# One encoder layer on one core: a fourth buffer for raw weights, two private buffer groups dissolved into general ones, and a new table of stage times

## The chip, the cores and the metric

The kernel runs on one core of a Trainium2 chip. Its time is the device time of one execution in microseconds, as the median of several runs. The kernel before took 1064.9, 1064.27 and 1064.7 us in three runs, so its median is 1064.7 us.

## The reference

One layer of a bidirectional encoder, on 512 positions of 1024 channels, all in float32. Two branches mix the tokens and a gated feed-forward part (FFN) follows:

```python
h = rmsnorm(x, mix_norm)
p = h @ w_in                                    # 1024 -> 9248 columns
rx, ry, qkv, z, ba, gates = split(p)
y_rnn = rglru_branch(rx, ry, ...) @ w_rnn_proj  # 12 blocks of 128 channels: convolution,
                                                # gates r and i by 128x128 weights, scans both ways
y_dn = deltanet_branch(qkv, z, ba, ...) @ w_dn_proj  # 8 heads, both directions, chunks with a
                                                # triangular solve and a carried state
g_rnn, g_dn = split(sigmoid(gates))
x = x + (g_rnn * y_rnn + g_dn * y_dn) @ w_out
h = rmsnorm(x, ffn_norm)
gt, up = split(h @ w_gate_up)                   # 2 x 2816 columns
x = x + (silu(gt) * up) @ w_down
return rmsnorm(x, final_norm)
```

## The kernel before

**Products.** TensorE (PE) does float32 products as products of two parts: every operand is split into a rounded part `hi` and a rest `lo`, and a tile of 128 output columns is the sum of hi·hi, lo·hi and hi·lo, three matmuls for each 128 input channels. For a weight tile this costs a transfer into a raw buffer (tag `wraw`, `NW` buffers of 4 KB per partition), a cast on ScalarE (ACT) to `hi`, and a subtraction on VectorE (DVE) for `lo` (`stage`, `weights`, `weights_k`). The tiles `whi` and `wlo` have two buffers each.

**Stages.** The program text runs through 229 stages: the norm and its transposes; tiles of `w_in`; the 12 RG-LRU blocks (`rg_front`, `rg_exp`, `rg_rest`, `rg_out`); four pairs of DeltaNet heads, each with `dn_front`, `dn_mats`, `dn_inverse`, `dn_state`, `dn_z` and `dn_out`; the two projections (`rnn_part`, `dn_part`); `w_out` (`out_mm`); the FFN in 22 pairs of tiles, of which the last 20 use a scheme with seven products of quarter size in place of eight; and the down projection.

`dn_inverse(g)` inverts small triangular blocks of pair `g`: a long chain of small DVE operations on a tile `X`, ended by a transpose into `tb[1]`, a subtraction from the identity, and a transpose into `tb[0]`. Small 32x32 matmuls on PE wait for that last transpose.

`down_sums(j)` serves the seven-product scheme of the down projection: for each of 11 `j` it loads two blocks of `w_down`, makes two sums on DVE and writes the result to DRAM (`sums`), from which it is read again much later. Its operands `r` and `b22` are tiles of tags `bg` and `bgb`, with two buffers each. In `rg_front` the weights of the RG-LRU gates come into `graw`, which has a single buffer.

**What sets the order.** Nothing is issued as the text runs. Every operation goes through a `Rec` object into a `Plan`, which is why nearly all rows of the profile carry line L379, the recorder's own. `Plan.order()` then deals the operations out to the five engines' queues by a simulated list schedule. An operation's priority is the time of its stage, `TIMES[s]` in tenths of a microsecond, plus its offset within the stage (loads of weights are put 40 or 20 us before their use, casts and subtractions `AHEAD` = 12 us). The operation of lowest priority whose inputs are ready, and for whose tiles the tag has a free buffer, is placed next. Stages past the end of the list `TIMES` follow the last entry at a spacing given by `spend`. So both the numbers of `TIMES` and the numbers of buffers (`N2` of 2 KB, tag `t2`; `N4` of 4 KB, tag `t4`; `NW`) decide the order on every engine, and the order is fixed when the program is built. On the chip each engine runs its list strictly in that order and waits where an input or a buffer isn't there.

Of the kernel before, what the change touches and what calls it, by code (L numbers as in the profile page):

```python
# [8 lines left out]
F32R = mybir.dt.float32r  # L9
# [5 lines left out]
P = 128  # L15
# [17 lines left out]
RELEASE = 200  # L33
LOOK = 40
TIMES = [
# [10 lines left out]
]  # L46
ENGINES = ("PE", "DVE", "ACT", "POOL", "SP")
N2, N4, NW = 14, 22, 3
AHEAD = 12.0
LASTK = 3  # L50
GATES = (0, 2, 4, 6, 16)
# [333 lines left out]
def trunk(ctx: ExitStack, tc: tile.TileContext, x, mix_norm, w_in, rg_conv_w, rg_conv_b, rg_wa, rg_ba, rg_wx, rg_bx,  # L385
# [9 lines left out]
    wp = ctx.enter_context(tc.tile_pool(name="wp", bufs=2))  # L395
# [10 lines left out]
    def nm(s):  # L406
        uid[0] += 1
        return f"{s}{uid[0]}"

    def new(pool, shape, tag, bufs, dt=F32):  # L410
        return plan.tile(pool, shape, dt, tag, bufs, nm(tag))
# [4 lines left out]
    def axb():  # L416
        return new(ps, (P, 512), "ax", 3)
# [4 lines left out]
    def two(dt=F32, shape=(P, 512)):  # L422
        return new(t2, shape, "t2", N2, dt)

    def four(dt=F32, shape=(P, 2, 512)):
        return new(t4, shape, "t4", N4, dt)
# [7 lines left out]
    def act(out_, in_, func, after=(), **kw):  # L434
        plan.extra = after
        A.activation(out_, in_, func, **kw)
        plan.extra = ()
# [6 lines left out]
    def f(ap):  # L444
        return ap.bitcast(F32)
# [112 lines left out]
    def pcol(i, j):  # L558
        return par[:, i, j:j + 1]
# [77 lines left out]
    def in_proj(col, po=None, admit=()):  # L637
        spend(5.2)
        hi, lo = (weights_k if len(first_tiles) < 3 else weights)(win[:, :, col:col + P], KD, P, admit)
        po = mmb() if po is None else po  # L640
        mm3(po, hi, lo, lambda k: hh[:, k, :], lambda k: hl[:, k, :], KD, 2 if len(first_tiles) < 3 else 1)
        first_tiles.append(col)
        return po

    def split(src, pair):
        A.copy(pair[:, 0, :], src)
        V.tensor_tensor(pair[:, 1, :], src, f(pair[:, 0, :]), ALU.subtract)

    def conv(po, w, bias, u):
        A.activation(u, po, AF.Identity, scale=w(2), bias=bias)  # L650
        V.scalar_tensor_tensor(u[:, 2:S], po[:, 0:S - 2], w(0), u[:, 2:S], ALU.mult, ALU.add)
        V.scalar_tensor_tensor(u[:, 1:S], po[:, 0:S - 1], w(1), u[:, 1:S], ALU.mult, ALU.add)
        V.scalar_tensor_tensor(u[:, 0:S - 1], po[:, 1:S], w(3), u[:, 0:S - 1], ALU.mult, ALU.add)
        return u
# [79 lines left out]
    def rg_front(b):  # L734
        u, us, r, i = two(), four(F32R), four(), four()
        po = in_proj(C_RX + b * P, admit=(u, us, r, i))
        graw, ghi, glo = new(wp, (P, 4, P), "graw", 1), two(F32R, (P, 4, P)), two(F32R, (P, 4, P))
        now = plan.t
        plan.t = now - (40 if b > 2 else 12)
        Q.dma_start(graw[:, 0:2, :], wa[:, b])  # L740
        Q.dma_start(graw[:, 2:4, :], wx[:, b])
        plan.t = now - AHEAD
        A.copy(ghi, graw)
        V.tensor_tensor(glo, graw, f(ghi), ALU.subtract)
        plan.t = now
        conv(po, lambda k: rg_w(k, b), rg_b(b), u)
        split(u, us)
        for q in range(4):
            d = q % 2
            pq = axb()  # L750
            T.matmul(pq, ghi[:, q, :], us[:, 0, :], start=True, stop=False)
            T.matmul(pq, ghi[:, q, :], us[:, 1, :], start=False, stop=False)
            T.matmul(pq, glo[:, q, :], us[:, 0, :], start=False, stop=True)
            act((r if q < 2 else i)[:, d, :], pq, AF.Sigmoid, bias=pcol(0, (O_BA if q < 2 else O_BX) + 12 * d + b))
        V.tensor_tensor(i, i, u.unsqueeze(1).to_broadcast([P, 2, S]), ALU.mult)
        return r, i
# [373 lines left out]
    def rg_group(bs):  # L1130
        nonlocal prev
        fr, m0 = marks(lambda: [rg_front(b) for b in bs])
        rg_flush()
        hs, m2 = rg_mid(bs, fr, m0)
        prev = (bs, hs, m2)
# [26 lines left out]
    def down_sums(j, after):  # L1162

        now = plan.t
        r, b22 = new(wp, (P, 2, 512), "bg", 2), new(wp, (P, 512), "bgb", 2)
        plan.extra = after
        Q.dma_start(r, wdn[:, j, 0, :].rearrange("p (h n) -> p h n", h=2))
        Q.dma_start(b22, wdn[:, j, 1, 512:D])
        plan.extra = ()
        V.tensor_tensor(r[:, 0, :], r[:, 0, :], r[:, 1, :], ALU.add)  # L1170
        V.tensor_tensor(r[:, 1, :], r[:, 1, :], b22, ALU.add)
        sums[j] = new(dr, (P, 2, 512), "sums", NF // 2)
        Q.dma_start(sums[j], r)
        plan.t = now
# [223 lines left out]
    for n in range(BRIDGE, NF):  # L1398
        if n - BRIDGE < NF // 2:
            down_sums(n - BRIDGE, last_split)  # L1400
        gate_up(n)
# [222 lines left out]
```

## Time and profile before

| what | value |
|---|---|
| runs | 1064.9, 1064.27, 1064.7 us, median 1064.7 us |
| span of the profiled execution (the only time the page gives for it) | 1066.3 us |
| TensorE busy | 1045.2 us, 98% of the span, 6731 matmuls |
| VectorE busy | 867.6 us, 81% |
| ScalarE busy | 675.7 us, 63% |
| GpSimd busy | 53.0 us, 5% |
| moved by DMA | 122.83 MB |

The profiled execution is 1.6 us (0.15%) longer than the median of the runs. Tile names in the profile come without their numbers, so `t` is any general tile (tags `t2` and `t4`), `mm`, `ax` and `st` are the three kinds of PSUM banks, and `hh`, `hl` the two parts of the normed input. A row of a timeline gives a start, the time taken by so many like instructions, and in brackets how long the engine had idled before them and for what. A row of the chain of waits is a piece of the chain that ended last. A row of a table of windows gives the length of a stretch and each engine's busy time in it.

### The profile page before, as it was taken

What the parts mean: (1) busy time and instruction counts of PE and PEld (TensorE: products, weight loads), DVE (VectorE), ACT (ScalarE), POOL (GpSimd) and SP (SyncE); (2) the same over time, 40 slices, a digit from 0 to 9 for tenths busy, and PEclk for the clock granted to TensorE, in tenths of its full rate; (3) what the DMA queues carried; (4) which work ended last, traced back from release to release, by engine and by line L of the source; (5) the groups of instructions that cost most, each with busy time, mean ns of one, the idle gap of its engine ahead of it and who ended that gap; (6) DMA issues with size and microseconds to landing.
All of it is one profiled execution on the core that took longest, in us unless ns stands there. A gap on an engine that the chain in (4) does not pass through costs nothing.

```text
span 1066.3 us, 17661 instructions
## 1 busy us (share of the span) xinstructions
PE 1045.2 (98%) x6731; PEld 908.7 (85%) x6731; DVE 867.6 (81%) x1606; ACT 675.7 (63%) x1244; POOL 53.0 (5%) x109
## 2 busy tenths in 40 slices
PE   8999999999999999999999999999999999999997
PEld 7888888887879887988788898889999999998876
DVE  7679899669966696599379567669989989889998
ACT  7997997878464856783874534447444544546664
POOL 2000000202000211110020000000000000000000
PEclk9999999999999999999999999999999999999999
DMA  8142333224331243223203222554577433325643
GB/s 254 45 119 79 102 85 91 68 86 124 104 109 33 83 125 91 58 73 99 71 15 96 79 103 80 183 168 149 178 229 246 129 102 104 113 93 197 193 137 113
DMA packets 174390, 122.83 MB, mean 115 GB/s; under 512 B 5953, under 2 KB 160721, under 8 KB 174305
## 3 DMA queue, kind: packets, MB, share of 16 engines
q1 hardware_dynamic: 172832, 118.41, 37.1%
q10 hardware_dynamic: 1184, 3.15, 0.8%
q8 instruction: 53, 0.87, 0.3%
q0 software_dynamic: 288, 0.13, 0.1%
q14 instruction: 33, 0.26, 0.1%
HBM read 113.78 MB, written 7.90 MB: 114 GB/s over the span
## 4 chain that ended last, share of the span: by engine, by line
PE 71%; DVE 14%; ACT 8%; issue 4%; DMA 3%; POOL 0%; SPq 0%; DVEq 0%; ACTq 0%; POOLq 0%
PE mm L379 43%; PE ax L379 18%; PE st L379 10%; DVE t L379 9%; ACT t L379 5%; DVE wlo L379 3%; ACT L379 1%; DVE na L379 1%; ACT whi L379 1%; ACT ax L379 1%; DMA wraw<-sums 1%; DMA wraw<-in_w_in_dram 1%; DMA wraw<-in_w_gate_up_dram 1%; DMA bg<-in_w_down_dram 1%; DVE hl L379 0%
## 5 line engine op out<-in xcount | busy, mean ns | idle before, releaser
L379 DVE TENSOR_TENSOR t<-t,t 128x512 fp32r<-128x512 f32 (+23 forms) x466 | 226.7, 501 | 14.8 <-ACT t L379 6.3
L379 PE MATMUL mm<-hh,whi 128*128 128x512 f32 (+2 forms) x648 | 229.4, 363 | 0.4 <-ACT hh L379 0.4
L379 PE MATMUL mm<-hl,whi 128*128 128x512 f32 (+2 forms) x648 | 228.9, 362 | 0.8 <-DVE hl L379 0.8
L379 ACT CAST whi<-wraw 128x1024 fp32r<-128x1024 f32 (+3 forms) x139 | 130.1, 937 | 155.2 <-PE mm L379 87.8
L379 DVE TENSOR_TENSOR wlo<-wraw,whi 128x1024 fp32r<-128x1024 f32 (+3 forms) x138 | 150.4, 1092 | 75.1 <-PE mm L379 27.4
L379 PE MATMUL mm<-hh,wlo 128*128 128x512 f32 (+1 forms) x632 | 146.8, 364 | 0.0
L379 PE MATMUL ax<-t,t 32*32 32x32 f32 (+3 forms) x1062 | 141.7, 288 | 2.9 <-issue 1.8
L379 PEld LDWEIGHTS mm<-hl,whi 128*128 128x128 f32 (+1 forms) x648 | 121.8, 188 | 18.5 <-DVE hl L379 1.2
L379 PEld LDWEIGHTS mm<-hh,whi 128*128 128x128 f32 (+1 forms) x648 | 121.7, 188 | 17.8 <-ACT hh L379 0.7
L379 PEld LDWEIGHTS ax<-t,t 128*128 128x128 f32 (+1 forms) x1062 | 109.5, 162 | 20.9 <-issue 4.6
L379 PEld LDWEIGHTS mm<-hh,wlo 128*128 128x128 f32 x632 | 109.1, 190 | 17.4
L379 ACT CAST t<-t 128x512 fp32r<-128x512 f32 (+2 forms) x128 | 80.9, 650 | 48.2 <-DVE t L379 42.9
L379 DVE SCALAR_TENSOR_TENSOR t<-mm,par,t 128x511 f32<-128x511 f32 (+1 forms) x108 | 80.3, 745 | 20.3 <-ACT t L379 19.0
L379 PE MATMUL mm<-t,t 128*128 128x256 f32 (+1 forms) x468 | 91.6, 337 | 0.8 <-DVE t L379 0.7
L379 ACT ACT_TABLE_LOAD x69 | 88.5, 1283 | 5.2 <-PEq L1610 1.7
L379 PE MATMUL mm<-t,whi 128*128 128x512 f32 x320 | 82.1, 395 | 0.5 <-ACT whi L379 0.5
L379 PEld LDWEIGHTS mm<-t,t 128*128 128x128 f32 x468 | 72.4, 190 | 11.1 <-DVE t L379 2.5
L379 PEld LDWEIGHTS mm<-t,whi 128*128 128x128 f32 x320 | 59.3, 188 | 12.7 <-ACT whi L379 0.7
L379 ACT CAST t<-wraw 128x1024 fp32r<-128x1024 f32 (+1 forms) x51 | 44.9, 881 | 29.0 <-DMA wraw<-in_w_gate_up_dram 11.2
L379 ACT ACTIVATE t<-t 128x128 f32<-128x128 f32 (+4 forms) x86 | 47.1, 559 | 24.9 <-DVE t L379 23.6
L379 DVE TENSOR_TENSOR t<-wraw,t 128x1024 fp32r<-128x1024 f32 (+1 forms) x51 | 51.7, 1016 | 6.1 <-ACT t L379 5.9
L379 PE MATMUL mm<-t,wlo 128*128 128x512 f32 x160 | 43.3, 394 | 0.0
(210 smaller groups left out, 1702.9 us busy)
## 6 DMA issues: line engine op xcount, KB each, us to landing
wraw<-in_w_in_dram SPq DMA_DIRECT2D x72, 512.0 KB, 3.8
wraw<-in_w_gate_up_dram SPq DMA_DIRECT2D x44, 512.0 KB, 4.2
wraw<-in_w_rnn_proj_dram SPq DMA_DIRECT2D x16, 384.0 KB, 3.6
bg<-in_w_down_dram SPq DMA_DIRECT2D x11, 512.0 KB, 4.1
sums<-bg SPq DMA_DIRECT2D x11, 512.0 KB, 4.7
wraw<-sums SPq DMA_DIRECT2D x11, 512.0 KB, 4.6
wraw<-in_w_down_dram SPq DMA_DIRECT2D x22, 256.0 KB, 3.0
wraw<-in_w_down_dram SPq DMA_DIRECT2D x11, 512.0 KB, 3.7
```

What stands on the lines that cost most here:

```text
L379: self.plan.add(e, lambda: real(*a, **kw), outs, ins, cost, tail, table)
```

## The change

Three numbers of buffers change and the table `TIMES` is replaced. The weights of the RG-LRU gates (`graw`) become general 2 KB tiles, and the operands of the weight sums (`bg`, `bgb`) general 4 KB and 2 KB tiles. In SBUF this frees 2 KB + 2 x 4 KB + 2 x 2 KB = 14 KB per partition, and one more `wraw` buffer (4 KB), two more `t4` (8 KB) and one more `t2` (2 KB) take up 14 KB. The table before has 159 entries for 229 stages; the new one has 229.

```diff
 TIMES = [
-    -153745, -118892, -151742, -141630, -118601, -110624, -115268, -33958, -18020, -66486, -73432, -37443, -49540,
...
+    -193727, -159384, -193730, -126073, -120235, -159028, -125968, -63810, -13198, -66391, -64154, -63637, -49334,
...
 ]
 ENGINES = ("PE", "DVE", "ACT", "POOL", "SP")
-N2, N4, NW = 14, 22, 3
+N2, N4, NW = 15, 24, 4
...
     def rg_front(b):
         u, us, r, i = two(), four(F32R), four(), four()
         po = in_proj(C_RX + b * P, admit=(u, us, r, i))
-        graw, ghi, glo = new(wp, (P, 4, P), "graw", 1), two(F32R, (P, 4, P)), two(F32R, (P, 4, P))
+        graw, ghi, glo = two(shape=(P, 4, P)), two(F32R, (P, 4, P)), two(F32R, (P, 4, P))
...
     def down_sums(j, after):
 
         now = plan.t
-        r, b22 = new(wp, (P, 2, 512), "bg", 2), new(wp, (P, 512), "bgb", 2)
+        r, b22 = four(), two()
```

No operation is added or dropped: PE has the same number of matmuls in its list before and after. What changes is the order on all engines. Three places follow; the names are tiles, with the number of the tile in the program text.

**VectorE at the end of the inverse of pair 1.** `t2611` is `X`, `t2612` the product `tmp`, `t2614` is `tb[1]` and `t2613` is `tb[0]`; `wlo` with another number belongs to the weights of some product. Before:

```order
L379 TENSOR_TENSOR t2611_691<-t2611_691,t2612_692 128x15
L379 STREAM_TRANSPOSE t2614_694<-t2611_691 128x32x16
L379 TENSOR_TENSOR t2614_694<-id3256_136,t2614_694 128x512
L379 TENSOR_TENSOR wlo805_885<-wraw803_883,whi804_884 128x1024
L379 STREAM_TRANSPOSE t2613_693<-t2614_694 128x512
```

Now:

```order
L384 TENSOR_TENSOR wlo801_881<-wraw799_879,whi800_880 128x1024
L384 TENSOR_TENSOR t2611_691<-t2611_691,t2612_692 128x15
L384 STREAM_TRANSPOSE t2614_694<-t2611_691 128x32x16
L384 TENSOR_TENSOR t2614_694<-id3256_136,t2614_694 128x512
L384 TENSOR_SCALAR n2705_785<-dssq699_779 128x8
L384 STREAM_TRANSPOSE t2613_693<-t2614_694 128x512
```

The subtraction for a weight tile of 128x1024 that stood between the subtraction from the identity and the last transpose is gone from there; a scalar operation on 128x8 stands there now, and a subtraction for another weight tile stands a little ahead.

**VectorE in the last part of the DeltaNet projection, ahead of `w_out`.** `t490` to `t493` hold the merged branches, `wlo1065` and `wlo1068` are the low parts of the first tiles of `w_out`, `t41086` and `t41089` those of its second half. Before, the stretch reads

```order
L379 TENSOR_TENSOR t491_171<-t491_171,t21018_1098 128x512
L379 TENSOR_TENSOR t41089_1169<-wraw1087_1167,t41088_1168 128x1024
L379 TENSOR_TENSOR t41019_1099<-t491_171,t41019_1099 128x512
L379 TENSOR_TENSOR wlo1065_1145<-wraw1063_1143,whi1064_1144 128x1024
L379 TENSOR_TENSOR t41092_1172<-wraw1090_1170,t41091_1171 128x1024
```

and the first of the 22 additions of the weight sums (`bg1163_1243<-bg1163_1243`) comes 26 rows further on, among the last rows of `w_out`. Now (`t41163`, `t41188` and `t41212` are the `r` of three sums):

```order
L384 TENSOR_TENSOR t491_171<-t491_171,t21018_1098 128x512
L384 TENSOR_TENSOR t41163_1243<-t41163_1243 128x512
L384 TENSOR_TENSOR t41163_1243<-t41163_1243,t21164_1244 128x512
L384 TENSOR_TENSOR t41019_1099<-t491_171,t41019_1099 128x512
L384 TENSOR_TENSOR t492_172<-t492_172,t2844_924 128x512
L384 TENSOR_TENSOR wlo1065_1145<-wraw1063_1143,whi1064_1144 128x1024
L384 TENSOR_TENSOR t492_172<-t492_172,t2989_1069 128x512
L384 TENSOR_TENSOR t41188_1268<-t41188_1268 128x512
L384 TENSOR_TENSOR t492_172<-t492_172,t21036_1116 128x512
L384 TENSOR_TENSOR t41188_1268<-t41188_1268,t21189_1269 128x512
```

The additions of the first sums have moved from the end of `w_out` and the FFN to between the splits of the merged branches; a third pair (`t41212`) follows two rows after these, ahead of `wlo1068`.

**PE at its first products.** `mm62` is the small tile of 32 columns of `w_in` (both parts, 64 columns), `mm105` and `mm120` are full tiles of 128 columns, and `ax33` to `ax36` take transposes of the input. Before:

```order
L379 MATMUL ax35_115<-ident1_81,t428_108 128x128
L379 MATMUL mm62_142<-hh19_99,whi61_141 64x256
L379 MATMUL mm105_185<-hh19_99,t4103_183 128x256
L379 MATMUL mm62_142<-hl20_100,whi61_141 64x256
L379 MATMUL mm62_142<-hh19_99,whi61_141 64x256
L379 MATMUL mm62_142<-hl20_100,whi61_141 64x256
L379 MATMUL ax36_116<-ident1_81,t421_101 128x128
```

Now:

```order
L384 MATMUL ax35_115<-ident1_81,t428_108 128x128
L384 MATMUL mm120_200<-hh19_99,t4118_198 128x256
L384 MATMUL mm120_200<-hl20_100,t4118_198 128x256
L384 MATMUL mm120_200<-hh19_99,t4118_198 128x256
L384 MATMUL mm120_200<-hl20_100,t4118_198 128x256
L384 MATMUL ax36_116<-ident1_81,t421_101 128x128
```

The first products come from one full tile alone, where before a small tile and a full one took turns.

23 rows, old and new, of the table TIMES are left out of this document.

## The prediction, made before the changed kernel ran

> **What bounds the kernel now.** I read the page first for the busy shares, then the table of windows by 100 us for where TensorE (PE) is not busy, then PE's timeline and the chain of waits at those places, and VectorE's (DVE's) timeline where the wait is on DVE.
>
> The page's head and the windows (length; then busy time of PE, its weight loads, DVE, ACT, POOL; clock; DMA share; GB/s):
>
> ```profile
> span 1066.3 us, 17661 instructions
> PE 1045.2 (98%) x6731; PEld 908.7 (85%) x6731; DVE 867.6 (81%) x1606; ACT 675.7 (63%) x1244; POOL 53.0 (5%) x109
> ...
> 0.00:100.00 100.00, 94.22 (x520) 80.92 (x521) 78.45 (x131) 83.18 (x129) 7.39 (x21) 1.00 0.45 128
> ...
> 400.00:500.00 100.00, 97.91 (x714) 82.82 (x713) 76.49 (x201) 64.63 (x149) 11.12 (x24) 0.98 0.29 80
> 500.00:600.00 100.00, 97.98 (x869) 82.21 (x868) 72.15 (x181) 66.10 (x151) 5.42 (x14) 1.00 0.24 65
> 600.00:700.00 100.00, 100.00 (x563) 83.92 (x563) 60.27 (x114) 40.84 (x79) 0.00 (x0) 1.00 0.36 112
> 700.00:800.00 100.00, 98.10 (x732) 93.44 (x730) 92.58 (x160) 55.79 (x102) 0.00 (x0) 1.00 0.59 189
> ...
> 1000.00:1066.00 66.00, 58.55 (x263) 47.39 (x261) 60.12 (x98) 40.35 (x66) 0.00 (x0) 0.96 0.41 136
> ```
>
> PE is the bound: it is busy for 1045.2 of 1066.3 us, and the change removes none of its matmuls. Only the other 21.1 us can be won. Of these 5.8 lie in the first 100 us and 7.45 in the last 66 (the tail behind the last matmuls); 2.1, 2.0 and 1.9 lie in the windows from 400, 500 and 700. A new order cannot make PE's own work shorter, so I look only at these waits, and at what may make new ones.
>
> The largest wait is at the end of the inverse of DeltaNet pair 1. PE's rows there, the wait in brackets (378.26 is the last product of `dn_mats`, on which the inverse starts), then DVE's at the same place, then windows across it:
>
> ```profile
> 378.26 1.02 PE L379 MATMUL ax<-t 128*128 128x256 f32 x4
> ...
> 415.67 0.39 PE L379 MATMUL mm<-hl,whi 128*128 128x512 f32 x1
> 418.15 0.75 PE L379 MATMUL ax<-t,na 32*32 32x32 f32 x64 [2.09 <-DVE t L379]
> ```
>
> ```profile
> 415.64 0.69 DVE L379 TENSOR_TENSOR t<-id,t 128x512 f32<-128x512 f32 x1
> 416.25 1.22 DVE L379 TENSOR_TENSOR wlo<-wraw,whi 128x1024 fp32r<-128x1024 f32 x1
> 417.39 0.70 DVE L379 STREAM_TRANSPOSE t<-t 128x512 f32<-128x512 f32 x1
> ```
>
> ```profile
> 415.60:418.10 2.50, 0.45 (x3) 0.03 (x1) 2.46 (x4) 0.80 (x2) 0.00 (x0) 1.00 0.00 0
> ...
> 419.20:420.90 1.70, 1.70 (x6) 1.16 (x4) 0.00 (x0) 1.68 (x6) 0.00 (x0) 0.54 0.94 280
> 420.90:422.60 1.70, 1.70 (x67) 1.24 (x66) 0.00 (x0) 0.32 (x2) 0.00 (x0) 0.50 0.00 0
> ```
>
> PE stood 2.09 us for the last transpose, and DVE put a weight subtraction of 1.22 us ahead of that transpose. Afterwards the granted clock is 0.54 and 0.50 for 3.4 us.
>
> **The change part by part.** The unit of PE's work, from the chain (a run of 24 matmuls of 512 columns, and one of 12 with 256), and of DVE's additions of 512 elements:
>
> ```profile
> 52.35 5.44 PE st L379 x24
> ...
> 790.01 1.44 PE mm L379 x12
> ```
>
> ```profile
> 653.80 0.69 DVE L379 TENSOR_TENSOR t<-t,t 128x512 f32<-128x512 f32 x1
> 654.41 0.68 DVE L379 TENSOR_TENSOR t<-mm,t 128x512 f32<-128x512 f32 x1
> ```
>
> So 5.44 / 24 = 0.227 us a matmul of 512, 1.44 / 12 = 0.120 of 256, and an addition takes 0.61 us of DVE's queue (start to start).
>
> *Pair 1.* The chain of the inverse ran from the end of the last product (about 379.3) to the last transpose's end at 418.1, 38.8 us. Between the two uses PE's list held 36.8 us of other matmuls, counted from the order with the units above. In the new order it holds 44.7 us, and the 1.22 us subtraction no longer stands ahead of the last transpose. Other DVE work that the order places inside the chain grows, from 30.2 to 32.2 us of busy time by the durations of like rows, so the chain may take 40.8; 3.9 us are then left over, and the stall goes. Its worth: the start of the 32x32 matmuls is 2.48 us behind the start before it, less 0.23 is 2.25; and 3.4 us at half clock do 1.7 us of work, so 1.7 us more. Together -4.0.
>
> By the Trainium skill ("TensorE: Matmul & The Clock Gate", section "What's actually happening") the clock falls only after an idle window of about 3.4 us and comes back after as long a busy one. The trace agrees with the half rate and the 3.4 us of it, but here the fall came after a gap of 2.1; by that rule the stall would have cost its own 2.25 us only, and the sum below would be 1.7 us higher.
>
> *The FFN.* The chain of waits and the windows from 740 us on show DVE full, then DVE starved by transfers, then PE short:
>
> ```profile
> 752.13 4.82 DMA sums<-bg
> 756.97 5.43 DMA bg<-in_w_down_dram
> ...
> 771.75 6.37 DMA wraw<-in_w_gate_up_dram
> ```
>
> ```profile
> 770.00:780.00 10.00, 10.00 (x86) 10.00 (x85) 8.07 (x15) 3.71 (x6) 0.00 (x0) 1.00 0.60 192
> 780.00:790.00 10.00, 8.76 (x71) 8.35 (x70) 10.00 (x20) 5.03 (x9) 0.00 (x0) 1.00 0.67 219
> 790.00:800.00 10.00, 9.35 (x79) 9.14 (x77) 9.12 (x18) 4.53 (x9) 0.00 (x0) 1.00 0.70 216
> ```
>
> The operand of a weight sum has two buffers before; its next load waits for the write of the sum before last, and DVE loses 1.93 us of the window from 770. PE then loses 1.24 + 0.65 = 1.89 us. With general buffers the loads aren't tied to two, and a fourth raw buffer lets a weight transfer start one tile earlier, so this starvation should go. But DVE is nearly full anyway: the windows from 700 have it at 92.58. In the new order three sums, 6 x 0.61 = 3.7 us of additions, run ahead of the FFN, and yet seven of the eleven sit in the 50 us from PE's position 730 to 780 (a position is PE's work ahead of it), where eight sat in 63 us before. I keep half of the loss: -1.0, between -1.9 and a loss that the second rival prices.
>
> *Ahead of `w_out`.* Those three sums cost something where they now stand: the second part's low parts and the first tiles of `w_out` queue behind them on DVE, and PE's last matmuls of the DeltaNet projection cover them thinly. PE has no wait from 600 to 700 before (100.00 of 100). The most is all six additions in the open, 3.7 us; the least is nothing, since DVE is busy for only 60.27 us of these 100. I take half, +1.8.
>
> *Small waits.* They stand in several places, one row each (the fourth is PE's own, without an engine it waits for):
>
> ```profile
> 168.70 1.20 PE L379 MATMUL mm<-t,whi 128*128 128x512 f32 x4 [0.48 <-ACT whi L379]
> ...
> 248.00 1.13 PE L379 MATMUL ax<-t 128*128 128x256 f32 x4 [0.66 <-DVE na L379]
> ...
> 363.14 0.66 PE L379 MATMUL ax<-ident,t 128*128 128x128 f32 x4 [0.21 <-ACT ax L379]
> ...
> 512.85 0.28 PE L379 MATMUL ax<-t,t 32*32 32x32 f32 x12 [1.79 <-issue]
> ...
> 1008.93 0.50 PE L379 MATMUL st<-wlo,t 128*128 128x512 f32 x1 [0.21 <-DVE wlo L379]
> ```
>
> The four on DVE and ACT make 0.48 + 0.66 + 0.21 + 0.21 = 1.6 us. The order behind them is new everywhere, so I count them gone, -1.6, and half as much new ones of the same kind, +0.8, since weights are now issued earlier ahead of their use. The 1.79 us in which PE waits for nothing the profile shows fell into one of four like bursts; whether it comes again can't be read from the order. Half of it: -0.9, between -1.8 and 0.
>
> *The start.* PE's rows before:
>
> ```profile
> 8.47 1.20 PE L379 MATMUL ax<-ident,t 128*128 128x128 f32 x9 [0.91 <-DVE t L379]
> 10.09 0.33 PE L379 MATMUL mm<-hh,whi 128*64 128x256 f32 x1 [0.41 <-ACT hh L379]
> ...
> 11.37 0.33 PE L379 MATMUL mm<-hl,whi 128*64 128x256 f32 x1 [0.83 <-DVE hl L379]
> ```
>
> the cast of the second full weight tile on ACT, and the page's transfer rate by slices of 26.7 us:
>
> ```profile
> 15.22 1.04 ACT L379 CAST t<-wraw 128x1024 fp32r<-128x1024 f32 x1
> ```
>
> ```profile
> GB/s 254 45 119 79 102 85 91 68 86 124 104 109 33 83 125 91 58 73 99 71 15 96 79 103 80 183 168 149 178 229 246 129 102 104 113 93 197 193 137 113
> ```
>
> Now one full tile feeds PE first, without the small tile. The second full tile comes behind nearly as many bytes as before (the two x loads, one full tile and one gate block), so its cast ends again near 16, but PE's list reaches its matmuls after 22 rows of the first tile where it had 39 rows before. 17 rows of about 0.12 are 2.0 us that PE lacks; against that, PE in its old order had waits of 0.41 and 0.83 for the first `hh` and `hl`, and while it waits for the tile those are no longer in the open. I take +1.0, between 0 and 2.0. Next, SP issues nine gate blocks of 256 KB ahead of the fifth full tile. With it 7 MB lie in the queue, which at the first slice's 254 GB/s are in by about 27 us; PE needs that tile at position 37, so nothing of it is in the open.
>
> *The sum:* -4.0 - 1.0 + 1.8 - 1.6 + 0.8 - 0.9 + 1.0 = -3.9 us, 1062.4 on the profiled execution of 1066.3. That execution is 1.6 above the median of the runs, 1064.7, so the forecast is 1060.8 us.
>
> **The rivals.** *The next inverse stalls instead.* Pair 2 in the trace of before (PE's last `dn_mats` product and first 32x32 matmuls, DVE's transpose between):
>
> ```profile
> 461.68 1.02 PE L379 MATMUL ax<-t 128*128 128x256 f32 x4
> ...
> 507.87 0.75 PE L379 MATMUL ax<-t,na 32*32 32x32 f32 x64
> ```
>
> ```profile
> 507.00 0.69 DVE L379 STREAM_TRANSPOSE t<-t 128x512 f32<-128x512 f32 x1
> ```
>
> The transpose ended at 507.69 and PE was there at 507.8: the chain took 45.0 us and PE's cover was 45.1. The new order leaves 42.9 us of cover. It also takes 2.7 us of other DVE work out of the chain, so it should take 42.3 and just fit, by 0.6. If it does not shrink, PE waits 2.1 us there and pays 1.7 at half clock: 1060.8 + 3.9 = 1064.7, no change. It decides as soon as the chain is over 42.9.
>
> *DVE becomes the bound in the FFN (slower).* Seven sums in 50 us are 14 additions, 8.5 us, on an engine whose work for the products alone fills PE's time. If no lead has been built up by position 730, the 8.5 us come into the open; before, 1.9 did. The term of -1.0 is then +6.6, and the time 1060.8 + 7.6 = 1068.4. For it: the window from 740 on, where DVE was on the chain with fewer sums per us; the sums' loads now share SP's queue and the general buffers with the weights, so a full pool holds both. Against it: three sums are done early, two more 4 KB tiles let DVE run ahead, and before, eight sums cost PE only 1.9 with starvation in it. It decides from where DVE stands without idle time while PE waits on `t`.
>
> *More is won.* If the early sums are hidden, the FFN's loss goes whole, the fetch gap stays away, the start is no worse and there are no new small waits, another 1.8 + 0.9 + 0.9 + 1.0 + 0.8 = 5.4 us go: 1055.4.
>
> *The stall goes but not its clock.* If the half rate from 419.2 to 422.6 has another cause than the gap, the first term is -2.3 and the time 1062.5. The rows speak against it, since the clock is 1.00 up to the gap, and of the windows of 100 us above only the one that holds it has less than 1.00 ahead of the tail. The rule of the Trainium skill's clock-gate page would have it so.
>
> **How the numbers follow.** The forecast's own case (1058 to 1063) gets 0.36, more won 0.17, the clock 0.07, pair 2 0.15, DVE in the FFN 0.25, the last because a whole new order has more places to lose than I can price. A measurement of this kernel can tell about 0.2%, 2.1 us, from no change, so faster means below 1062.6 and slower above 1066.8. Faster: nearly all of the first (0.34), 0.17, and 0.05 of the clock's case: 0.56. Slower: 0.25. The rest, 0.19, is pair 2's case and the edges. The range reaches from 1055.0, where more is won, to 1069.5, a little past the slower case, as its price may be a sum more (1.2); the likeliest case's own range is 1058 to 1063.
>
> **What would show it.** In the profile of the changed kernel: no wait over 0.5 us at the first 32x32 matmuls of any pair, and no window below 0.9 of the clock after the start; windows from 700 with PE over 99; a wait of up to 2 us around `w_out`; the first 100 us with PE about 1 us below 94.22. I am wrong if PE is short in the FFN with DVE at 10.00 of 10, if an inverse of another pair stalls over 2 us, or if the start loses several us to the gate blocks.

## The result, and the profile after

The changed kernel took 1056.79 us (median of 6 runs, 1055.64 to 1057.59) against 1064.72 before (6 runs): 7.9 us less, a ratio of 0.9927 with a 95% interval of 0.9913 to 0.9941. The forecast was 1060.8, so the direction was right and the size half of what came. One execution of the kernel before, among those that the experiments are compared with, took 1288.92 us at a granted clock of 0.752 and is in no comparison.

The page's head, and the windows of 100 us (length, then busy time of PE, its weight loads, DVE, ACT, POOL, clock, DMA share, GB/s) of the changed kernel, whose recorder stands at L384 (at L370 in some kernels below):

```profile
span 1055.8 us, 17690 instructions
PE 1042.7 (99%) x6731; PEld 909.3 (86%) x6731; DVE 868.2 (82%) x1606; ACT 676.9 (64%) x1245; POOL 61.4 (6%) x109
...
0.00:100.00 100.00, 94.82 (x515) 80.74 (x516) 74.39 (x125) 85.44 (x135) 6.73 (x21) 1.00 0.50 139
...
400.00:500.00 100.00, 99.95 (x728) 84.42 (x727) 73.41 (x195) 68.34 (x145) 9.15 (x20) 1.00 0.30 82
500.00:600.00 100.00, 99.74 (x876) 83.24 (x874) 72.39 (x178) 69.30 (x157) 6.38 (x14) 1.00 0.23 63
600.00:700.00 100.00, 99.49 (x560) 83.37 (x559) 69.68 (x132) 41.34 (x79) 0.00 (x0) 1.00 0.52 170
700.00:800.00 100.00, 100.00 (x777) 97.13 (x776) 98.14 (x168) 58.49 (x107) 0.00 (x0) 1.00 0.56 182
```

From 100 to 1000 us PE now stands for 0.82 us in all: 0.05, 0.26 and 0.51 in three windows, while the other six read 100.00. In the prediction's profile the same nine windows left 7.57 us. What remains is the first 100 us (5.18 idle) and the tail.

At the end of pair 1's inverse the wait is gone. PE's row of the first 32x32 matmuls there, and DVE's rows of the transposes before it:

```profile
418.44 0.75 PE L384 MATMUL ax<-t,na 32*32 32x32 f32 x64
```

```profile
411.03 0.69 DVE L384 TENSOR_TENSOR t<-id,t 128x512 f32<-128x512 f32 x1
411.64 0.16 DVE L384 TENSOR_SCALAR n<-dssq 128x8 f32<-128x8 f32 x1
411.76 0.71 DVE L384 STREAM_TRANSPOSE t<-t 128x512 f32<-128x512 f32 x1
```

The transpose ends at 412.47 and PE comes for it at 418.44, with 6.0 us left over and no bracket on its row. In the FFN DVE has 9.97 to 10.00 of 10 in every window from 730 to 800 and PE loses nothing:

```profile
770.00:780.00 10.00, 10.00 (x86) 10.00 (x85) 10.00 (x19) 5.05 (x9) 0.00 (x0) 1.00 0.57 185
780.00:790.00 10.00, 10.00 (x86) 10.00 (x85) 10.00 (x19) 5.64 (x10) 0.00 (x0) 1.00 0.55 180
```

The new waits over 0.2 us that I find are two at the start, one in the burst at 508, and this one ahead of `w_out`:

```profile
672.61 0.73 PE L384 MATMUL ax<-whi,t 128*128 128x512 f32 x2 [0.51 <-ACT t L384]
```

### The profile page after: what moved, and what is told of

Read it like the earlier page. It is cut to its first block, busy times and chain, and to the rows that moved or that the text cites. A ratio compares the mean times of both kernels' runs of the same rounds, so it can differ in the third digit from the quotient of the medians.

```text
span 1055.8 us, 17690 instructions
## 1 busy us (share of the span) xinstructions
PE 1042.7 (99%) x6731; PEld 909.3 (86%) x6731; DVE 868.2 (82%) x1606; ACT 676.9 (64%) x1245; POOL 61.4 (6%) x109
## 4 chain that ended last, share of the span: by engine, by line
PE 96%; DMA 1%; ACT 1%; DVE 1%; issue 0%; ACTq 0%; SPq 0%; DVEq 0%
PE mm L384 57%; PE ax L384 24%; PE st L384 15%; ACT t L384 1%; DMA wraw<-in_w_in_dram 1%; DMA wraw<-in_w_out_dram 1%; DVE na L384 0%; DVE t L384 0%; DVE wlo L384 0%; ACTq L384 0%; ACT L384 0%; ACT rst L384 0%; SPq L384 0%; ACT hh L384 0%; DVE hl L384 0%
## 5 line engine op out<-in xcount | busy, mean ns | idle before, releaser
L384 DVE TENSOR_TENSOR t<-t,t 128x512 fp32r<-128x512 f32 (+22 forms) x489 | 242.9, 506 | 29.6 <-ACT t L384 18.5
L384 PE MATMUL mm<-hh,whi 128*128 128x512 f32 (+2 forms) x648 | 228.8, 363 | 0.0
L384 PE MATMUL mm<-hl,whi 128*128 128x512 f32 (+2 forms) x648 | 228.4, 362 | 0.0
L384 ACT CAST whi<-wraw 128x1024 fp32r<-128x1024 f32 (+3 forms) x139 | 130.1, 937 | 128.4 <-PE mm L384 60.5
L384 DVE TENSOR_TENSOR wlo<-wraw,whi 128x1024 fp32r<-128x1024 f32 (+3 forms) x138 | 151.3, 1096 | 59.4 <-ACT whi L384 29.3
L384 PE MATMUL mm<-hh,wlo 128*128 128x512 f32 (+1 forms) x632 | 146.6, 364 | 0.0
L384 PE MATMUL ax<-t,t 32*32 32x32 f32 (+3 forms) x1062 | 138.4, 285 | 0.3 <-issue 0.3
L384 PEld LDWEIGHTS mm<-hh,whi 128*128 128x128 f32 (+1 forms) x648 | 121.6, 188 | 17.0
L384 PEld LDWEIGHTS mm<-hl,whi 128*128 128x128 f32 (+1 forms) x648 | 121.6, 188 | 16.9
L384 ACT CAST t<-t 128x512 fp32r<-128x512 f32 (+2 forms) x140 | 88.7, 650 | 56.0 <-DVE t L384 50.7
L384 PEld LDWEIGHTS ax<-t,t 128*128 128x128 f32 (+1 forms) x1062 | 109.6, 159 | 17.4 <-issue 2.1
L384 PEld LDWEIGHTS mm<-hh,wlo 128*128 128x128 f32 x632 | 108.6, 189 | 17.3 <-issue 0.2
L384 DVE SCALAR_TENSOR_TENSOR t<-mm,par,t 128x511 f32<-128x511 f32 (+1 forms) x108 | 80.0, 742 | 13.0 <-ACT t L384 11.9
L384 PE MATMUL mm<-t,t 128*128 128x256 f32 (+1 forms) x468 | 89.9, 336 | 0.0
L384 PE MATMUL mm<-t,whi 128*128 128x512 f32 x320 | 81.7, 395 | 0.0
L384 PEld LDWEIGHTS mm<-t,t 128*128 128x128 f32 x468 | 72.8, 190 | 8.9 <-DVE t L384 0.2
L384 PEld LDWEIGHTS mm<-t,whi 128*128 128x128 f32 x320 | 59.3, 188 | 12.4 <-ACT whi L384 0.4
L384 ACT CAST t<-wraw 128x1024 fp32r<-128x1024 f32 (+1 forms) x51 | 44.6, 880 | 26.3 <-DMA wraw<-in_w_gate_up_dram 8.8
L384 ACT ACTIVATE t<-t 128x128 f32<-128x128 f32 (+4 forms) x86 | 46.9, 558 | 22.4 <-DVE t L384 20.9
L384 DVE TENSOR_TENSOR t<-wraw,t 128x1024 fp32r<-128x1024 f32 (+1 forms) x51 | 51.2, 1006 | 2.5 <-ACT t L384 2.4
L384 POOL TENSOR_SCALAR_AFFINE_SELECT t<-t 128x512 f32<-128x512 f32 x32 | 33.1, 1042 | 163.9 <-DMA t<-gcr 103.2
```

The lines of the kernel that those rows point to most:

```text
L384: self.plan.add(e, lambda: real(*a, **kw), outs, ins, cost, tail, table)
```

## The experiments

Twelve runs followed. Gains over the kernel before are against its runs on the same chip, whose median was 1064.49, 1065.31 and 1063.77 us in the three sets; its single runs lie up to 3.6 us away. Losses against the changed kernel are against its median of 1056.79, taken in a set of its own, so they carry the 1.5 us by which the sets differ.

**The kernel before, profiled again** (no edit).

> The kernel before, unchanged, profiled a second time, to see which of its waits stand in every execution. Theory A (all waits follow from the order): the same waits within 0.3 us, 2.25 at pair 1 with half a clock behind it, 2.6 us in the FFN from 785 to 822, 1.8 with no releaser in the burst at 511. Theory B (waits for transfers vary, those on engines don't): pair 1 and the burst again, the FFN's anywhere from 0.3 to 3 us; the span then differs from 1066.3 by up to 4 us.

1064.32 us, at a span of 1062.6. Its rows at pair 1 and in the FFN:

```profile
417.57 0.75 PE L379 MATMUL ax<-t,na 32*32 32x32 f32 x64 [1.49 <-DVE t L379]
```

```profile
418.00:420.00 2.00, 2.00 (x60) 1.42 (x52) 0.00 (x0) 1.98 (x6) 0.00 (x0) 1.00 0.95 258
420.00:422.00 2.00, 2.00 (x70) 1.72 (x63) 0.00 (x0) 1.81 (x6) 0.00 (x0) 1.00 0.04 11
...
760.00:770.00 10.00, 9.53 (x80) 9.32 (x79) 8.91 (x16) 4.68 (x9) 0.00 (x0) 1.00 0.73 237
770.00:780.00 10.00, 10.00 (x86) 10.00 (x85) 8.42 (x16) 4.89 (x9) 0.00 (x0) 1.00 0.72 225
780.00:790.00 10.00, 8.96 (x72) 8.56 (x72) 10.00 (x19) 5.01 (x10) 0.00 (x0) 1.00 0.73 234
```

Neither theory as written. The wait at pair 1 is 1.49 where it was 2.09, and the clock behind it is 1.00 where it was 0.54 and 0.50. The FFN loses 0.47 + 1.04 = 1.5 us, at 760 as well as at 780, with DVE short of work (8.91, 8.42) as before. So the first profile, on which the prediction stood, shows an execution with more lost than usual: half a clock that this one doesn't have, and 3.7 us more of span.

**One row moved at pair 1** (in the kernel before, behind the list schedule):

```diff
         todo = plan.order()
+        low = ...    # DVE's row that writes wlo805
+        last = ...   # DVE's last transpose of pair 1, t2613
+        todo.insert(last, todo.pop(low))
```

> The kernel before, with one row moved: on VectorE the weight subtraction that stood ahead of the last transpose of pair 1's inverse now stands behind it. The wait of 2.25 us shrinks by 1.13 to about 1.1 us. Theory A (a gap of 2 us trips the clock, one of 1 us does not): 1.1 + 1.7 = 2.8 us less, 1061.9 us, clock at 1.00 behind the gap. Theory B (the half clock comes with any gap there, or has another cause): 1.1 us less, 1063.6, clock still near 0.5 for 3.4 us.

1062.78 us, ratio 0.9985 [0.9975, 0.9995]: 1.6 us less. PE's wait and the clock behind it:

```profile
416.15 0.75 PE L379 MATMUL ax<-t,na 32*32 32x32 f32 x64 [0.46 <-DVE t L379]
```

```profile
418.00:420.00 2.00, 2.00 (x71) 1.47 (x70) 0.00 (x0) 1.89 (x7) 0.00 (x0) 1.00 0.75 209
```

The interval (0.5 to 2.7) holds theory B's 1.1 us, the length of the row put ahead; theory A's 2.8 lies just outside it. The clock of 1.00 behind the wait decides nothing, since the second profile of before has it at 1.00 too; half a clock may be won in some executions.

**A third buffer for the weight sums**, in the kernel before:

```diff
-        r, b22 = new(wp, (P, 2, 512), "bg", 2), new(wp, (P, 512), "bgb", 2)
+        r, b22 = new(wp, (P, 2, 512), "bg", 3), new(wp, (P, 512), "bgb", 1)
```

> The kernel before with three buffers for the first operand of the weight sums in place of two (and one for the second in place of two): its order differs only in the FFN, where SP issues those loads earlier. If the two buffers starve VectorE in the FFN: 1 to 2 us less, 1062.5 to 1063.5, and VectorE at 10.0 of 10 in the windows from 760 and 770. If VectorE's own work is what PE waits for there: no change within 0.7 us.

1062.34 us, ratio 0.9982 [0.9971, 0.9993]: 1.9 us less by the ratio. The windows:

```profile
760.00:770.00 10.00, 10.00 (x86) 10.00 (x85) 10.00 (x19) 5.13 (x9) 0.00 (x0) 1.00 0.72 236
770.00:780.00 10.00, 10.00 (x86) 10.00 (x85) 9.35 (x17) 5.02 (x9) 0.00 (x0) 1.00 0.74 234
780.00:790.00 10.00, 10.00 (x84) 9.93 (x84) 10.00 (x19) 5.03 (x9) 0.00 (x0) 1.00 0.75 242
```

PE is at 10.00 here although DVE still does every addition, and it is so from 740 to 830. DVE has 9.35 in the window from 770, where 10.0 was expected. From 740 to 800 it waits 0.6 us for transfers, for a raw weight, where the two profiles of before have 3.2 and 2.8 us, of them 1.3 and 1.2 for the sums' operand. But the profile alone doesn't show the repair. The kernel with the one row moved has the FFN's order and the two buffers of before, and PE loses next to nothing in it:

```profile
770.00:780.00 10.00, 10.00 (x85) 10.00 (x85) 9.20 (x17) 4.95 (x10) 0.00 (x0) 1.00 0.67 219
780.00:790.00 10.00, 9.98 (x83) 9.78 (x82) 10.00 (x19) 4.99 (x9) 0.00 (x0) 1.00 0.73 236
```

So the FFN's loss differs between executions of the same order, with how late the transfers land: 1.9, 1.5 and 0.2 us in three. That the third buffer takes it away rests on the run times.

**Both repairs together**, the two edits above in one kernel.

> The kernel before with the two local repairs together: the row moved at pair 1 and the third buffer for the weight sums' first operand. Theory A (the gain is a sum of separate waits): the two gains measured singly add, 1.7 + 2 = 3.7 us less than before, and about half of the change's 7.9 us is then explained by two places; the small waits (168, 247, 363, the burst at 511) stand as they were. Theory B (a wait removed is given back at the next one, since other engines come no sooner): 2.5 us or less.

1062.36 us, ratio 0.9984 [0.9973, 0.9995]: 1.7 us less, where 3.7 was expected of a plain sum. In its profile the FFN is at 10.00 from 760 to 790, and pair 1 waits 1.16 us; its chain on DVE ran as long as in the first profile of before, 0.7 us more than in the kernel with the one row moved. Single differences of 1 to 2 us are at the edge of what these runs tell apart (0.5 to 2.9 here, 0.7 to 3.1 and 0.5 to 2.7 singly). The 3.7 lies outside the interval, so theory B's figure (2.5 or less) is the nearer one; but with the two single intervals as wide as they are, that the gains add is neither shown nor excluded. What is shown is that they don't make 7.9.

**The old table with the new buffers:**

```diff
 TIMES = [
-    -193727, -159384, -193730, -126073, -120235, -159028, -125968, -63810, -13198, -66391, -64154, -63637, -49334,
...
+    -153745, -118892, -151742, -141630, -118601, -110624, -115268, -33958, -18020, -66486, -73432, -37443, -49540,
...
 N2, N4, NW = 15, 24, 4
```

> The old table of 159 stage times with the new numbers of buffers and the general tiles. If the buffers bring the gain (the FFN's starvation, earlier weights): the FFN's loss of 1.9 us goes, others with it, 1060 or less. If the new table brings it and the buffers only make room for it: no gain, 1064 to 1075, since the old numbers were chosen for the old buffers; waits of PE of the same sort as before, at other places.

1092.8 us, ratio 1.0263 [1.024, 1.0285]: 28 us slower, more than either theory allowed. Four of its waits on PE:

```profile
74.14 2.38 PE L379 MATMUL ax<-t,t 128*128 128x512 f32 x9 [2.67 <-ACT t L379]
78.05 0.96 PE L379 MATMUL ax<-t,t 128*128 128x512 f32 x3 [1.53 <-ACT t L379]
84.05 0.79 PE L379 MATMUL mm<-hh,whi 128*128 128x512 f32 x1 [5.04 <-ACT whi L379]
...
180.83 0.80 PE L379 MATMUL st<-hh,whi 128*128 128x512 f32 x1 [7.98 <-ACT t L379]
```

In all four PE waits for ScalarE. In the first 200 us PE is idle for 24.3 us, where it was 6.4 before, and the granted clock is 0.95. ScalarE has no more to do than before (675.5 us of work against 675.7, 69 table loads of 1.28 us in both), and from 70 to 85 us it works without a pause. So its order differs and not its work. My reading, not tested further: with more buffers the list schedule can place operations earlier and does, and ScalarE's queue then holds what PE needs behind what it doesn't. The new table can't be run without the buffers: with 14 tiles of 2 KB or 22 of 4 KB, or in the kernel before as it stands, the list schedule finds no order for it at all. A table fitted anew to the old buffers was not tried.

**Three raw buffers**, in the changed kernel: `N2, N4, NW = 15, 24, 3`.

> The changed kernel with three buffers for raw weights in place of four, the rest as changed. If the fourth buffer carries the gain: 1061 to 1065. If it only lets weights come earlier than they are needed: within 2 us of 1056.8, but every order behind the first weight wait may move, so some new waits of 0.5 to 2 us may show in PE's rows.

1062.67 us, 5.9 us above the changed kernel's median; the profiled execution, its fastest, is 3.8 us longer than the changed kernel's. Up to 650 us PE has the waits of the changed kernel and no other over 0.6 us, and pair 1 keeps its 6 us; the loss comes later, of which these rows:

```profile
696.43 3.93 PE L384 MATMUL mm<-t,t 128*128 128x512 f32 x16 [0.78 <-DVE t L384]
...
719.18 0.39 PE L384 MATMUL st<-hl,whi 128*128 128x256 f32 x1 [0.40 <-DVE hl L384]
...
1008.69 1.65 PE L384 MATMUL ax<-t,t 128*128 128x512 f32 x6 [0.51 <-DVE na L384]
```

They stand behind `w_out` and in the down projection. This is a table fitted to four buffers run with three, so it bounds the fourth buffer's worth from above.

**The table moved at random**, each entry by up to 1.0 us (two draws) and by up to 0.2 us, for instance in the first entries of the first draw and of the small one:

```diff
 TIMES = [
-    -193727, -159384, -193730, -126073, ...
+    -193733, -159376, -193738, -126075, ...
+    -193726, -159382, -193729, -126072, ...
 ...
```

> The changed kernel with each of the 229 stage times moved by a random amount of up to 1.0 us either way. If the gain is in buffers and in the broad order: within 1.5 us of 1056.8. If it is in the fit of the single numbers, which decide which operation wedges itself ahead of which: 3 to 10 us slower, 1060 to 1067, with waits of PE at places that have none now.

> The changed kernel with each stage time moved by up to 1.0 us, other random numbers than the first time (which cost 4.8 us). If the fit of the single numbers carries the gain: again 2 to 8 us slower than 1056.8, with new waits at other places. If the first time was an unlucky draw: within 1.5 us.

> The changed kernel with each stage time moved by up to 0.2 us, less than one addition of 512 elements on VectorE. If the order hangs on such small differences: 1 to 4 us slower. If not: within 1 us of 1056.8.

1061.56 us and 1066.1 us with 1.0 us, 1057.16 with 0.2: 4.8 and 9.3 us slower, and 0.4, which is no difference these runs can tell. The new waits are on single rows, of the first draw and of the second:

```profile
638.58 1.65 PE L370 MATMUL mm<-t,whi 128*128 128x512 f32 x6 [1.48 <-ACT whi L370]
...
764.34 1.70 PE L370 MATMUL ax<-t,t 128*128 128x256 f32 x12 [1.05 <-DVE t L370]
```

```profile
597.28 1.02 PE L370 MATMUL ax<-t,t 32*32 32x32 f32 x96 [1.03 <-ACT t L370]
599.60 0.30 PE L370 MATMUL ax<-t,na 64*64 64x64 f32 x2 [1.30 <-ACT t L370]
600.99 1.41 PE L370 MATMUL ax<-t,na 64*64 64x64 f32 x30 [1.09 <-ACT t L370]
```

Moving single numbers by up to a microsecond thus costs 4.8 to 9.3 us, where the whole change brought 7.9; the buffers and the broad order without the fit don't hold the gain. In the second draw it is an inverse, pair 3's, whose small steps wait behind other work on ScalarE. The clock falls behind these three waits as well, to about 0.5 for some 7 us; by estimate, half of the time in which PE works there, that is 3 of the 9.3 us:

```profile
600.00:602.00 2.00, 1.01 (x29) 1.04 (x30) 0.00 (x0) 1.93 (x6) 0.00 (x0) 0.91 0.02 4
602.00:604.00 2.00, 1.70 (x10) 1.04 (x6) 1.23 (x1) 1.24 (x2) 0.00 (x0) 0.50 0.00 0
```

**A wait of chosen length at pair 2**, in the changed kernel (5 in place of 3 for the second):

```diff
         for i in todo:
             plan.ops[i][1]()
+            if slow and i == slow[0][0]:    # the subtraction from the identity of pair 2
+                for _ in range(3):
+                    slow[0][1]()            # the same subtraction into an unused tile
```

> The changed kernel with three extra subtractions of 512 elements (into a tile that nobody reads) on VectorE ahead of the last transpose of pair 2's inverse, where 0.35 us were left over: PE waits 1.83 - 0.35 = 1.5 us there. If a gap of about 2 us is needed to trip the clock: clock 1.00 behind it. If 1.5 is enough: near 0.5 for some 3.4 us.

> As the one with three, with five extra subtractions: PE waits 3.05 - 0.35 = 2.7 us at pair 2. By the case of pair 1 before (2.25 us and half the clock behind it) the clock falls to near 0.5 for some 3.4 us, 1.7 us lost. If only an idle stretch of 3.4 us trips it: clock 1.00.

Spans of 1058.0 and 1059.9 us, 2.2 and 4.1 over the changed kernel's 1055.8 (single executions; the changed kernel's six run from 1053.8 to 1055.8). PE's row and the windows behind it, first with three extra operations, then with five (a row of windows ends in clock, DMA share, GB/s):

```profile
506.08 0.74 PE L384 MATMUL ax<-t,na 32*32 32x32 f32 x64 [1.95 <-DVE t L384]
```

```profile
506.00:508.00 2.00, 1.92 (x68) 1.66 (x69) 1.83 (x3) 1.94 (x6) 0.00 (x0) 0.81 0.05 8
508.00:510.00 2.00, 2.00 (x76) 1.26 (x77) 0.00 (x0) 1.34 (x4) 0.00 (x0) 0.50 0.00 0
```

```profile
508.07 1.08 PE L384 MATMUL ax<-t,na 32*32 32x32 f32 x64 [3.37 <-DVE t L384]
```

```profile
508.00:510.00 2.00, 1.93 (x66) 1.80 (x67) 1.82 (x3) 1.94 (x5) 0.00 (x0) 0.50 0.04 8
510.00:512.00 2.00, 2.00 (x11) 1.06 (x16) 0.00 (x0) 1.43 (x5) 0.00 (x0) 0.50 0.00 0
512.00:514.00 2.00, 2.00 (x99) 1.84 (x99) 0.00 (x0) 0.78 (x3) 0.00 (x0) 0.50 0.03 8
```

The waits came out longer than meant (1.95 for 1.5, 3.37 for 2.7), since the extra operations took 2.14 and 3.60 us, not 1.83 and 3.05. The clock fell behind both, for about 3.5 us and for over 6. Of the other profiles' single waits, it fell behind one of 2.09 us and stayed at 1.00 behind 1.49, behind 1.55 (the kernel with the third buffer), 1.75 (at 676 us in the next experiment) and 1.79 us (the burst before), one profile each.

But the length of one wait doesn't decide it. In the second draw above three waits of 1.03, 1.30 and 1.09 us, within 5 us of each other, brought it down. And with the old table and the new buffers it was still at 1.00 for more than 4 us behind the wait of 2.67 us, until the waits of 1.53 and 5.04 us followed:

```profile
76.00:78.00 2.00, 0.52 (x3) 0.09 (x1) 2.00 (x3) 1.97 (x2) 0.00 (x0) 1.00 0.00 0
78.00:80.00 2.00, 0.96 (x3) 0.49 (x3) 2.00 (x3) 1.96 (x3) 0.00 (x0) 0.90 0.00 0
```

These rows look as if PE's idle share over a stretch of some microseconds counts, and where that stretch begins; no run here tests that.

**One row moved ahead of `w_out`**, in the changed kernel:

```diff
+        low = ...    # DVE's row that writes t41086, a tile of w_out's second half
+        half = ...   # the second addition of the first weight sum, t41163
+        todo.insert(half, todo.pop(low))
```

> The changed kernel with one row moved on VectorE: the subtraction for a tile of w_out's second half, which waits for a cast that waits for a late transfer, goes behind one addition of the merged branch and the two additions of the first weight sum. If PE's wait of 0.5 us near 672 comes from that blocked head of the queue: it goes, 0.5 to 0.7 us less. If it comes from the early sums' additions taking VectorE's time: it stays within 0.2 us, since as many additions run as before.

1057.34 us against 1056.79: no gain that these runs can tell. The wait at 672 is gone, and a longer one stands 4 us later. PE's row, and DVE's two rows ahead of it:

```profile
676.65 0.50 PE L384 MATMUL ax<-wlo,t 128*128 128x512 f32 x1 [1.75 <-DVE wlo L384]
```

```profile
671.70 0.69 DVE L384 TENSOR_TENSOR t<-t 128x512 f32<-128x512 f32 x1 [2.27 <-DMA t<-in_w_down_dram]
...
673.04 1.22 DVE L384 TENSOR_TENSOR t<-wraw,t 128x1024 fp32r<-128x1024 f32 x1
```

Both theories missed. DVE's queue now stops for 2.27 us at the addition itself, whose operand has not landed, and the tile for `w_out` waits behind it. In these rows the blocked head of the queue is the mechanism, but there are two late transfers, and the fitted order had the earlier one in front. How late they are differs between executions: the two kernels with a longer wait at pair 2 have the changed kernel's order here, and PE waits 0.65 us at this place in one of them and not at all in the other.

## Why the prediction was right, and where it was off

**The base.** "That execution is 1.6 above the median of the runs" was wrong. An execution's time is its span and 1.7 us or so more: the changed kernel's profiled run reads 1057.59 at a span of 1055.8, the second profile of before 1064.32 at 1062.6. The execution of 1066.3 us thus took about 1068.0, 3.3 over the median. The terms were read from an execution with that much more in it, and taken off the median. The forecast's sum, -3.9, stands against 7.9 between the medians, and against 10.5 between the profiled spans, of which 3.7 is what the two profiles of before differ by.

**Pair 1** (-4.0). The mechanism held: chain 38.7 us (predicted up to 40.8), cover 44.7 as counted. The size held for the profile it was read from, 2.25 + 1.7; in the second profile it is 1.65 us (start to start; 1.49 by the row), with the clock at 1.00, and repairing 1.1 us of it brought 1.6 by the times. So for a usual execution this term was too large by some 2 us. One profile can't tell what a wait usually costs.

**The FFN** (-1.0, half kept because "DVE is nearly full anyway"). This step failed. The loss went whole: from 700 to 800 DVE has 98.14 of 100 in the changed kernel and PE 100.00, so a nearly full DVE costs PE nothing here. The loss came with DVE's waits for transfers (3.2 and 2.8 us in the two profiles with a loss, 0.8 and 0.6 in the ones without). My reading is that an engine at 10.00 that began ahead stays ahead, so what counts is its work against PE's over the whole stretch; the slower rival's 8.5 us of additions did not come into the open. That rival (0.25) was the wrong reading of the same window. The prediction's row is read too narrowly as well: the 1.93 us that DVE lost from 770 were a wait for a raw weight of the gate-up product, and not for the sums' operand:

```profile
778.14 0.69 DVE L379 TENSOR_TENSOR t<-wraw,wraw 128x512 f32<-128x512 f32 x1 [1.93 <-DMA wraw<-in_w_gate_up_dram]
```

**Ahead of `w_out`** (+1.8). The place was right, the price 0 to 0.65 in three profiles, the reason wrong: not six additions in the open but late transfers. The chain of waits of the changed kernel has the transfer of `w_out` that landed last, with 6.3 us; loads of that size take 3.8 and 4.2 us in the page of before. That the early sums' operands, loaded at the same time, delay it is my reading:

```profile
662.62 6.29 DMA wraw<-in_w_out_dram
```

**Small waits** (-1.6 + 0.8). The old ones went as assumed; nearly no new ones came outside the start and `w_out`, so the +0.8 was too much. They differ between executions: the second profile of before has one of 0.6 us, start to start, at pair 0's first 32x32 matmuls, where the first has none. In the changed kernel no window from 100 to 400 is below 100.00.

**The burst without a releaser** (-0.9). It stood in all five profiles with the old order on PE, with 1.49 to 1.79 us in the bracket, so it seems to belong to the order; what PE waits for there stays open. The changed kernel has 0.26 there:

```profile
508.09 0.32 PE L384 MATMUL ax<-t,t 32*32 32x32 f32 x17 [0.26 <-issue]
```

**The start** (+1.0). The place was right, the loss isn't there. The changed kernel's 94.82 is 0.6 us more than the 94.22 of the prediction's profile and 0.5 us less than the second profile of before:

```profile
0.00:100.00 100.00, 95.34 (x523) 82.03 (x524) 78.97 (x131) 83.29 (x130) 7.17 (x21) 1.00 0.47 130
```

In five profiles of the old order PE is idle for 4.4 to 5.8 us of these 100, and for 4.3 to 5.2 us in four of the new one (the changed kernel, the two with a longer wait at pair 2, and the one with a row moved ahead of `w_out`). The wait for the first `hl` stays, 0.90 us at 10.98, where the prediction counted it as covered. The new waits are the one foreseen on the second full tile, at 0.22 us, and one more on `hl`:

```profile
13.94 0.38 PE L384 MATMUL mm<-hl,t 128*128 128x256 f32 x1 [0.50 <-DVE hl L384]
...
15.99 0.39 PE L384 MATMUL mm<-hh,t 128*128 128x256 f32 x1 [0.22 <-ACT t L384]
```

**The rivals.** Pair 2 was decided by 0.35 us: chain 42.6 against a cover of 42.9, where 42.3 was expected. That it fit is in part luck. The kernels with a longer chain show what stood on the other side, the wait and half a clock. The case "more is won" (1055.4, at 0.17) is the one that came, nearly whole. The clock's rule from the Trainium skill ("TensorE: Matmul & The Clock Gate", section "What's actually happening"), an idle window of about 3.4 us, does not fit as it stands: the clock fell behind single waits of 1.95 and 2.09 us, and behind three of 1.03 to 1.30. Its half rate fits, and its length of about 3.4 us fits behind the two single waits; behind 3.37 us and behind the three it was about twice that.

**The signs.** Of what was to show it, the inverses without a wait, the clock, the FFN and the wait ahead of `w_out` came as written; the first 100 us below 94.22 did not.

**The whole.** From 100 to 1000 us the waits fell from 7.57 us in the first profile of before, or 6.80 in the second, to 0.82. Nearly all went, where the sum kept back half of several and set aside 2.8 us for losses at `w_out` and at the start, of which 0.65 at most came; that is why the forecast was 4.0 us too high. That it came no further off is in part luck, since pair 1, too large for a usual execution, made up for some of this. Of 7.9 us, the two places repaired singly account for 1.6 and 1.9, and 1.7 together as measured; the rest, by difference, is in the waits of 0.2 to 2 us along the program, and none of the edits tried carries it. That the buffers alone don't bring it is shown (28 us slower), and so is that moving the table by a microsecond costs 5 to 9 us. What the buffers are worth with a table of their own stays open.

## What to carry to other kernels

When an order is fitted to a planner, more buffers alone may make it worse, here by 28 us, so fit the order anew with every change of buffers. Before pricing a wait from one profile, set that execution's own time against the other runs (here the span and 1.7 us), read more than one profile, and ask of each wait whether an engine or a transfer ends it. And a full engine beside the bounding one is no loss in itself: look for the windows in which it is idle while the other will wait for it later.

## What was not expected of the hardware

The clock's fall behind short waits: to about 0.50 for 3.4 us after 2.09 us, for some 3.5 after 1.95, for over 6 after 3.37 and for some 7 after three of 1.03 to 1.30 close together, and 1.00 after single ones of 1.49 to 1.79 and for 4 us after one of 2.67. And the pause of TensorE in a burst of 96 32x32 matmuls, 1.49 to 1.79 us with no releaser in one order and 0.26 in another with as many matmuls.
